# Sums over features as two float32r products, and 64-row products of two heads in turns, in a two-block transformer kernel

## The chip, the cores and the metric

The program runs on one core of a Trainium2 chip. The metric is the device time of one execution in microseconds, the median over runs. A profile of one execution gives the rows below: TensorE is PE (its weight loads PEld), VectorE is DVE, ScalarE is ACT, GpSimd is POOL, and SP issues most of the loads.

## What is computed

Two transformer blocks on 512 tokens of 1024 features, all in float32. Block one is a differential attention with 8 heads, a modulation from a condition vector, and a mixture of 16 experts. Block two is a forgetting attention beside an RWKV-7 recurrence (8 heads of 64), a merge of the two, and a product-key expert layer. What bears on the change:

```python
# block one, per head: rmsnorm over the 128 features of the head
o = rmsnorm(o, subln_g) * (1.0 - lam_init)
# block one: condition rows
mod = cond @ ada_w[i] + ada_b[i]
# block two, recurrence, per head of 64: key norm, bonus, group norm
kk = kk / jnp.maximum(jnp.sqrt(jnp.sum(kk * kk, axis=-1, keepdims=True)), 1e-12)
bonus = jnp.sum(r_h * k_h * r_k.reshape(H, N), axis=-1, keepdims=True) * v_h
mu = jnp.mean(y, axis=-1, keepdims=True)
var = jnp.mean(jnp.square(y - mu), axis=-1, keepdims=True)
```

## The kernel before

Large products are made of three float32r products: each operand is split into a head (`split` L53: an ACT copy that rounds to float32r, L57) and a rest (a DVE subtraction, L58), and `mm3` (L47 to L51) multiplies head by head, rest by head and head by rest. A float32 product is one call, and the trace shows it as two TensorE instructions.

A sum over features is a product with a constant matrix, because features lie on the partitions: `ones` (128 by 128) or `bones` and `bswap` (two blocks of 64 by 64). There are 32 such products of 128 by 512 in float32, each followed by an operation that reads the sum from PSUM:

- `head_norm` (L376): after each of the 8 attention heads, ACT squares the head (L378, tile `sq`), PE sums it (L380), ACT takes logarithm and exponential into `rn` (L382, L383), DVE multiplies (L384) and `rn` is split into `on`, the input of the output projection. The head itself waits in the only PSUM buffer of kind `d` until L384 has read it.
- `ada_end` (L178): 8 sums of half rows of `g1`, `A2`, `B2` and `g2` (L184), read by ACT (L186) or DVE (L188). `g1` is called in the middle of the first half of the output projection (L491), the other three behind it (L499). `A2` and `B2` go through DRAM to the columns that the router uses (L538 to L540, L550).
- `rwkv`, first loop, for each of 4 pairs of heads: the key norm (L1354) and the bonus (L1385).
- `rwkv`, last loop, for each pair: mean (L1562) and variance (L1569) of `y`.

The first loop of `rwkv` (L1346 to L1430) prepares chunks of 32 tokens. Per pair and head, 16 products of 64 by 64 by 64 (L1414, `p` of PSUM kind `a`, which has three buffers) go to DVE masks (L1416, L1417), then to 16 products of 32 rows (L1428). The 16 products read the 64 partitions of their head, and write the lower and the upper 64 partitions of the bank in turns. After the last pair the masked matrices go through DRAM to a triangular recursion on DVE (L1468). Its setting up reuses the loop's memory (L1432 to L1442).

The chain over chunks (L1532) multiplies for both heads in turns (L1537), head 0 from rows 0 to 63 into the lower half and head 1 from rows 64 to 127 into the upper half of one tile. The last loop (L1545) has 15 products of 64 by 64 by 32 for one head and then 15 for the other, into the two halves of one bank (L1553), with one step of the merge's products (`fill(1, fox)`) behind each head; then `y` (L1558, two buffers), the two sums, the scaling (L1570 to L1575) and the split into `yrT`. The loads of `gt` and `bo` for the next pair (L1547, L1548) have one buffer each. Another float32 product with all four quarters of the array in turns is L1522.

No order is written by hand around these places: the tile framework orders the instructions of each engine by program order and by when it reckons them ready, gives tiles of one `tag` the same buffers, and lets a new tile of a tag wait until the one before it is released. PE runs its list in order. `fill` hands it steps of other products between.

Of the kernel before, what the change touches and what calls it, by code (L numbers as in the profile page):

```python
# [27 lines left out]
class Kern:  # L28
# [24 lines left out]
    def split(self, hl, src, scale=None, eng=None):  # L53
# [5 lines left out]
        else:  # L59
            nc.scalar.activation(hl[0], src, AF.Copy, scale=scale)  # L60
            nc.vector.scalar_tensor_tensor(hl[1], src, scale, hl[0].bitcast(F32), OP.mult, OP.subtract)

    def pair(self, pool, shape, tag, bufs=None):
        return [self.t(pool, shape, F32R, tag + s, bufs) for s in ("_hi", "_lo")]
# [45 lines left out]
    def constants(self, cp):  # L110
        nc, I = self.nc, self.I
        self.ident = self.t(cp, [128, 128], F32, "ident")
        nc.vector.memset(self.ident, 0.0)
        nc.gpsimd.affine_select(self.ident, self.ident, pattern=[[-1, 128]], compare_op=OP.not_equal, fill=1.0,
                                base=0, channel_multiplier=1)
        self.ones = self.t(cp, [128, 128], F32, "ones")
        nc.vector.memset(self.ones, 1.0)
        self.cols = self.t(cp, [128, I["cols"].shape[1]], F32, "cols")
        nc.sync.dma_start(self.cols, I["cols"])
        self.acols = self.t(cp, [128, 3 * KC], F32, "acols")  # L120
        nc.sync.dma_start(self.acols, I["acols"])
# [55 lines left out]

    def ada_end(self, dst, gain=None):  # L178

        nc = self.nc  # L180
        for h in range(2):
            s = slice(h * 512, h * 512 + 512)
            p = self.ps(kind="b")
            nc.tensor.matmul(p, self.ones, dst[:, s], start=True, stop=True)  # L184
            if gain is None:
                nc.scalar.activation(dst[:, s], p, AF.Copy)  # L186
            else:
                nc.vector.scalar_tensor_tensor(dst[:, s], p, 1.0, gain[:, s], OP.add, OP.mult)  # L188
# [18 lines left out]
    def mixer1(self):  # L207
        nc, I, tc = self.nc, self.I, self.tc
        with ExitStack() as ph:
# [166 lines left out]
            def head_norm(h, po):  # L376
                sq = self.t(sp, [128, T], F32, "sq", 1)
                nc.scalar.activation(sq, po, AF.Square)  # L378
                pss = self.ps(kind="b")
                nc.tensor.matmul(pss, self.ones, sq, start=True, stop=True)  # L380
                rn = self.t(sp, [128, T], F32, "rn", 1)
                nc.scalar.activation(rn, pss, AF.Ln, bias=epsc, scale=1.0 / 128)  # L382
                nc.scalar.activation(rn, rn, AF.Exp, scale=-0.5)  # L383
                nc.vector.scalar_tensor_tensor(rn, po, gcol, rn, OP.mult, OP.mult)  # L384
                self.split([z[:, h, :] for z in on], rn)
# [94 lines left out]
            nf = nf.rearrange("p a b -> p (a b)")  # L480
            def residual(pool, p, t, h):
                hs = slice(h * 512, (h + 1) * 512)
                y = self.t(pool, [128, 512], F32, "ry", 1)
                nc.vector.tensor_tensor(y, p, self.g1[:, hs], OP.mult)
                nc.vector.tensor_tensor(xr[:, t, hs], xr[:, t, hs], y, OP.add)
# [3 lines left out]
            for kc in range(KC):  # L489
                if kc == 4:  # L490
                    self.ada_end(self.g1)  # L491
                if kc == KC - 1:
                    head_norm(7, po)
                    self.dump("on", on[0].bitcast(F32))
                for t in range(NT):
                    ts = slice(t * 128, (t + 1) * 128)
                    self.mm3(py[t], [z[:, kc, ts] for z in on], [z[:, kc % 2, :] for z in ws[kc // 2]], kc == 0, kc == KC - 1)
            for d, gain in ((self.A2, nf), (self.B2, None), (self.g2, None)):
                self.ada_end(d, gain)  # L499
            for t in range(NT):  # L500
                residual(wo0, py[t], t, 0)
            self.close_right("m1wo")
# [3 lines left out]
            with tc.tile_pool(name="m1wo1", bufs=1) as op:  # L506
                ws = [wout(wp, op, kc, 1, 4) for kc in (0, 2, 4, 6)]
                for t in range(NT):
# [6 lines left out]
                    self.router_half(xr, t, 0)  # L515
                    residual(op, p, t, 1)
                    self.router_half(xr, t, 1)
# [725 lines left out]
    def rwkv(self, xT, yfT, wp):  # L1243
# [11 lines left out]
        with self.rw as ph:  # L1255
# [8 lines left out]
            BA = [self.t(ba, [128, 2, 8, 96], F32, "BA%d" % i) for i in range(4)]  # L1264
            bones, bswap = (self.t(one, [128, 128], F32, "bones%d" % i) for i in range(2))
            for m, i in ((bones, 0), (bswap, 64)):
# [8 lines left out]
            with ExitStack() as sub:  # L1275
# [70 lines left out]
                for hp in range(4):  # L1346
# [6 lines left out]
                    p = self.ps()  # L1353
                    nc.tensor.matmul(p, bones, sq, start=True, stop=True)  # L1354

# [28 lines left out]
                    p = self.ps()  # L1384
                    nc.tensor.matmul(p, bswap, r, start=True, stop=True)  # L1385
                    nc.vector.tensor_tensor(r, p, v, OP.mult)
# [6 lines left out]
                    for n, src in (("bk", bk), ("ar", ar), ("v", v2)):  # L1393
                        for i in range(2):
# [12 lines left out]
                            else:  # L1407
                                nc.vector.tensor_copy(Vr[:, ps_, :], p)
                    for g in range(2):
                        gs, vs = slice(g * 64, (g + 1) * 64), slice(64 - g * 64, 128 - g * 64)  # L1410
                        p = self.ps([128, 8, 2, C])
                        for j in range(16):
                            o = j % 2 * 64
                            nc.tensor.matmul(p[o:o + 64, j // 2], bk[gs, j].rearrange("p i t -> p (i t)"), ar[gs, j].rearrange("p i t -> p (i t)"), start=True, stop=True,  # L1414
                                             tile_position=(g * 64, o))
                        nc.vector.tensor_tensor(AI[g][:, :, 0, :], p[:, :, 0, :], m2[:, 0:1, :].to_broadcast([128, 8, C]), OP.mult)  # L1416
# [34 lines left out]
            def fill(n, steps):  # L1451
                for _ in zip(range(n), steps):
                    pass
# [91 lines left out]
            for hp in range(4):  # L1545
# [3 lines left out]
                p = self.ps([128, 16, C], "c")  # L1549
                for g in range(2):  # L1550
                    gs, vs = slice(g * 64, (g + 1) * 64), slice(64 - g * 64, 128 - g * 64)
                    for j in range(1, 16):
                        nc.tensor.matmul(p[vs, j, :], MW[hp][gs, j - 1, 64:128], rT[gs, hp, j, :], start=True, stop=True,  # L1553
                                         tile_position=(g * 64, 64 - g * 64))
                    fill(1, fox)
                y = self.t(sp, [128, T], F32, "y", 2)
# [481 lines left out]
```

## Time and profile before

| | |
|---|---|
| median of 3 runs | 2536.67 us (2530.67 to 2538.79) |
| the profiled execution | 2533.18 us |
| its span, first to last instruction | 2531.5 us |
| mean granted TensorE clock | 0.982 of full speed |
| PE busy | 2418.7 us, 96% |
| DVE, ACT, POOL busy | 1925.4, 1123.1, 545.8 us |

The last 1271 us are the product-key layer, which the change leaves alone. The places above lie at these times of the span: heads 120 to 286 us, condition rows and output projection 286 to 312, first loop of the recurrence 860 to 978, triangular recursion from 978, chain over chunks 1100 to 1136, last loop 1135 to 1184. A busy PE means that some product is in flight, and the recorded length of a product overlaps the next; what a product costs the queue is the distance of its start to the start of the next.

### The profile page before, as it was taken

How to read it: one execution, taken by the hardware profiler on the slowest of the kernel's cores; microseconds unless marked ns; L12 is line 12 of the kernel's file. 1: busy time of each engine (PE TensorE's matmuls, PEld its weight loads, DVE VectorE, ACT ScalarE, POOL GpSimd, SP SyncE). 2: the span in 40 equal slices, each digit the busy share in tenths (PEclk: the TensorE clock that was granted, in tenths of full speed). 3: DMA queues.
4: the chain of work that ended last, by engine and by line, in shares of the span. 5: the costliest groups of instructions: out<-in, count | busy, mean ns of one | idle time of the engine just before them, and what ended most of it. 6: DMA issues, size and time to landing. Idle time of an engine off the chain costs nothing.

```text
span 2531.5 us, 36170 instructions
## 1 busy us (share of the span) xinstructions
PE 2418.7 (96%) x13502; PEld 1982.1 (78%) x13502; DVE 1925.4 (76%) x3698; ACT 1123.1 (44%) x1651; POOL 545.8 (22%) x456
## 2 busy tenths in 40 slices
PE   8999989999899999999999999989999899999998
PEld 5766766666567687777789989988888789888887
DVE  5577669898866657646689999948787688888886
ACT  3466547777534543223434445533333233333333
POOL 2010112223311100000000000024544434454440
PEclk9999989999999999998999999999999999999999
DMA  7343269999731122213343338799999899999992
GB/s 266 117 172 112 93 223 334 361 369 368 254 104 42 60 77 74 76 55 121 115 140 119 118 103 316 288 385 328 350 347 325 311 332 325 343 333 350 336 330 78
DMA packets 224248, 566.31 MB, mean 224 GB/s; under 512 B 27755, under 2 KB 75924, under 8 KB 223174
## 3 DMA queue, kind: packets, MB, share of 16 engines
q1 hardware_dynamic: 173218, 387.53, 43.5%
q0 software_dynamic: 46048, 166.73, 18.6%
q10 hardware_dynamic: 4804, 9.72, 1.0%
q8 instruction: 107, 1.75, 0.3%
q14 instruction: 71, 0.58, 0.1%
HBM read 511.99 MB, written 51.92 MB: 223 GB/s over the span
## 4 chain that ended last, share of the span: by engine, by line
issue 17%; PE 17%; DVE 10%; POOL 8%; DMA 3%; ACT 0%; POOLq 0%; DVEq 0%; ACTq 0%
POOL row L1765 8%; DMA row<-in_v,ix 2%; PE psu L49 2%; PE psu L51 2%; PE psu L50 2%; PE psx L1750 2%; PE py L50 1%; PE py L51 1%; PE py L49 1%; DVE u_lo L58 1%; PE psb L49 1%; PE psb L51 1%; PE psb L50 1%; DVE eq L1718 1%; DVE ti L1663 1%
## 5 line engine op out<-in xcount | busy, mean ns | idle before, releaser
L49 PE MATMUL psu<-x4T_hi,u_hi 128*128 128x384 f32 x1024 | 346.5, 339 | 5.3 <-ACT act L1815 4.4
L51 PE MATMUL psu<-x4T_hi,u_lo 128*128 128x384 f32 x1024 | 344.4, 337 | 2.3 <-DVE u_lo L58 2.3
L50 PE MATMUL psu<-x4T_lo,u_hi 128*128 128x384 f32 x1024 | 344.1, 336 | 0.0
L50 PE MATMUL py<-v_lo,W_hi 128*128 128x512 f32 x768 | 303.3, 395 | 13.3 <-DVE v_lo L58 13.3
L49 PE MATMUL py<-v_hi,W_hi 128*128 128x512 f32 x768 | 302.1, 393 | 5.8 <-ACT W_hi L57 4.4
L51 PE MATMUL py<-v_hi,W_lo 128*128 128x512 f32 x768 | 302.6, 394 | 4.0 <-DVE W_lo L58 4.0
L57 ACT ACTIVATE W_hi<-act 128x384 fp32r<-128x384 f32 x128 | 66.4, 525 | 395.1 <-DVE act L1899 395.1
L58 DVE TENSOR_TENSOR ew_lo<-ew_raw,ew_hi 128x2048 fp32r<-128x2048 f32 x93 | 216.7, 2331 | 28.4 <-ACT ew_hi L57 28.3
L1765 POOL DMA_INDIRECT row<-in_v,ix x128 | 183.3, 1432 | 220.1 <-DVE x L1781 188.6
L1765 POOL DMA_INDIRECT row<-in_u,ix x128 | 180.7, 1411 | 221.5 <-DVE dots L1772 203.2
L57 ACT ACTIVATE w_hi<-w_raw 128x1024 fp32r<-128x1024 f32 (+1 forms) x103 | 101.9, 992 | 226.3 <-PE psb L50 148.9
L57 ACT ACTIVATE u_hi<-u_raw 128x1024 fp32r<-128x1024 f32 x128 | 135.0, 1057 | 149.3 <-PE psu L50 132.6
L49 PEld LDWEIGHTS psu<-x4T_hi,u_hi 128*128 128x128 f32 x1024 | 193.1, 189 | 9.6 <-ACT act L1815 4.7
L50 PEld LDWEIGHTS psu<-x4T_lo,u_hi 128*128 128x128 f32 x1024 | 193.2, 189 | 3.7
L57 ACT ACTIVATE ew_hi<-ew_raw 128x2048 fp32r<-128x2048 f32 x93 | 178.1, 1916 | 39.2 <-PE psa L51 38.1
L51 PEld LDWEIGHTS psu<-x4T_hi,u_lo 128*128 128x128 f32 x1024 | 192.9, 188 | 2.9 <-DVE u_lo L58 2.8
L1772 DVE CUSTOM_DVE_ANT_0 row<-row,x 128x1024 f32<-128x1024 f32 x128 | 153.2, 1219 | 45.4 <-DMA row<-in_u,ix 45.3
L50 PEld LDWEIGHTS py<-v_lo,W_hi 128*128 128x128 f32 x768 | 145.8, 190 | 46.1 <-DVE v_lo L58 18.6
L58 DVE TENSOR_TENSOR v_lo<-v_raw,v_hi 128x1024 fp32r<-128x1024 f32 x128 | 156.2, 1221 | 33.0 <-ACT v_hi L57 33.0
L1781 DVE SCALAR_TENSOR_TENSOR x<-row,rg,x 128x1024 f32<-128x1024 f32 x128 | 164.0, 1281 | 17.6 <-DMA row<-in_v,ix 15.9
L51 PEld LDWEIGHTS py<-v_hi,W_lo 128*128 128x128 f32 x768 | 146.1, 190 | 35.9 <-DVE W_lo L58 5.6
L49 PEld LDWEIGHTS py<-v_hi,W_hi 128*128 128x128 f32 x768 | 145.7, 190 | 34.7 <-ACT W_hi L57 4.8
(662 smaller groups left out, 5455.0 us busy)
## 6 DMA issues: line engine op xcount, KB each, us to landing
u_raw<-in_uT SPq DMA_DIRECT2D x128, 512.0 KB, 6.1
v_raw<-in_v SPq DMA_DIRECT2D x128, 512.0 KB, 6.5
ew_raw<-in_wgate SPq DMA_DIRECT2D x32, 1024.0 KB, 7.3
ew_raw<-in_wup SPq DMA_DIRECT2D x32, 1024.0 KB, 7.7
ew_raw<-in_wdown SPq DMA_DIRECT2D x32, 1024.0 KB, 9.7
gd<-Gs SPq DMA_DIRECT2D x6, 4096.0 KB, 13.1
G<-gd SPq DMA_DIRECT2D x32, 768.0 KB, 8.8
w_raw<-in_w2b SPq DMA_DIRECT2D x39, 512.0 KB, 3.5
```

The lines of the kernel that those rows point to most:

```text
L49: mm(out, L[0], R[0], start=start, stop=False)
L50: mm(out, L[0], R[1], start=False, stop=False)
L51: mm(out, L[1], R[0], start=False, stop=stop)
L57: nc.scalar.activation(hl[0], src, AF.Copy)
L58: (eng or nc.vector).tensor_tensor(hl[1], src, hl[0].bitcast(F32), OP.subtract)
L1663: nc.vector.max_index(idx[:, 8:16], vals[:, 8:16], rest)
L1718: nc.vector.tensor_tensor(e4, e4, tf[:, s, :, :, None].to_broadcast([128, NT, 16, 16]), OP.mult)
L1750: nc.tensor.matmul(p[:, u, :], A[j], B[i][j], start=i == 0, stop=i == 1)
L1765: keep(nc.gpsimd.indirect_dma_start(r, None, I[name], bass.IndirectOffsetOnAxis(ap=ix[:, h, j:j + 1], axis=0)))
L1772: keep(nc.vector.tensor_tensor_reduce(r, r, x[:, t, :], 1.0, 0.0, OP.mult, OP.add, dots[:, h, j:j + 1]))
L1781: keep(nc.vector.scalar_tensor_tensor(x[:, t, :], r, g[:, h, j:j + 1], x[:, t, :], OP.mult, OP.add))
```

## The change

The sums become two float32r products, of the head and of the rest of the summed operand, with constants held as float32r (`ones_r`, and `bones` and `bswap` themselves). `halves` makes the two parts in buffers of tags that are there already (`rn`, `km`, `r`, `sq`, `kk`) or new (`sql`, `yh`, `yl`), one buffer each. To make room for `sql`, the scratch of the first four `residual` calls moves from the pool of the weights to tag `a`. The products L1414 and L1553 of the two heads of a pair are issued in turns; for L1414 the upper and lower output halves of head 1 are swapped in order, so that neighbours share neither rows nor columns, and both heads' PSUM tiles are open at once. The two steps of `fill` in the last loop come behind both heads.

```diff
+    def halves(self, pool, x, tags):
+        hl = [self.t(pool, [128, T], F32R, tag, 1) for tag in tags]
+        self.split(hl, x)
+        return hl
+    def sums(self, out, m, hl):
+        self.nc.tensor.matmul(out, m, hl[0], start=True, stop=False)
+        self.nc.tensor.matmul(out, m, hl[1], start=False, stop=True)
...
+        self.ones_r = self.t(cp, [128, 128], F32R, "ones_r")
+        nc.vector.tensor_copy(self.ones_r, self.ones)
...
-            nc.tensor.matmul(p, self.ones, dst[:, s], start=True, stop=True)
+            self.sums(p, self.ones_r, self.halves(pool, dst[:, s], ("rn", "sql")))
...
-                nc.tensor.matmul(pss, self.ones, sq, start=True, stop=True)
+                self.sums(pss, self.ones_r, self.halves(sp, sq, ("rn", "sql")))
...
-                residual(wo0, py[t], t, 0)
+                residual(sp, ("a", 2), py[t], t, 0)
...
-                    nc.tensor.matmul(p, bones, sq, start=True, stop=True)
+                    self.sums(p, bones, self.halves(sp, sq, ("km", "r")))
...
-                    nc.tensor.matmul(p, bswap, r, start=True, stop=True)
+                    self.sums(p, bswap, self.halves(sp, r, ("sq", "kk")))
...
+                    pg = [self.ps([128, 8, 2, C]) for _ in range(2)]
+                    for j in range(16):
+                        for g in range(2):
+                            gs, i = slice(g * 64, (g + 1) * 64), j ^ g
+                            o = i % 2 * 64
+                            nc.tensor.matmul(pg[g][o:o + 64, i // 2], bk[gs, i].rearrange("p i t -> p (i t)"), ar[gs, i].rearrange("p i t -> p (i t)"), start=True, stop=True,
+                                             tile_position=(g * 64, o))
                     for g in range(2):
...
-                        p = self.ps([128, 8, 2, C])
-                        for j in range(16):
-                            o = j % 2 * 64
-                            nc.tensor.matmul(p[o:o + 64, j // 2], bk[gs, j].rearrange("p i t -> p (i t)"), ar[gs, j].rearrange("p i t -> p (i t)"), start=True, stop=True,
-                                             tile_position=(g * 64, o))
...
-                for g in range(2):
-                    gs, vs = slice(g * 64, (g + 1) * 64), slice(64 - g * 64, 128 - g * 64)
-                    for j in range(1, 16):
+                for j in range(1, 16):
+                    for g in range(2):
+                        gs, vs = slice(g * 64, (g + 1) * 64), slice(64 - g * 64, 128 - g * 64)
                         nc.tensor.matmul(p[vs, j, :], MW[hp][gs, j - 1, 64:128], rT[gs, hp, j, :], start=True, stop=True,
                                          tile_position=(g * 64, 64 - g * 64))
-                    fill(1, fox)
+                fill(2, fox)
...
-                nc.tensor.matmul(p, bones, y, start=True, stop=True)
+                self.sums(p, bones, self.halves(sp, y, ("yh", "yl")))
...
-                nc.tensor.matmul(p, bones, sq, start=True, stop=True)
+                self.sums(p, bones, self.halves(sp, sq, ("yh", "yl")))
```

## Rows read from the trace of the kernel before

**Rows 1.** The page's first part: busy time and share of each engine.
```profile
PE 2418.7 (96%) x13502; PEld 1982.1 (78%) x13502; DVE 1925.4 (76%) x3698; ACT 1123.1 (44%) x1651; POOL 545.8 (22%) x456
```

**Rows 2.** Busy time by stretch: length, each engine, granted clock, DMA share, GB/s.
```profile
120.00:286.00 166.00, 162.39 (x876) 113.17 (x875) 121.86 (x293) 108.61 (x219) 12.83 (x19) 0.98 0.39 137
286.00:312.00 26.00, 26.00 (x97) 17.90 (x97) 12.81 (x18) 9.94 (x15) 6.16 (x21) 1.00 0.15 25
860.00:978.00 118.00, 118.00 (x988) 92.09 (x987) 65.61 (x103) 55.55 (x92) 4.04 (x12) 1.00 0.24 77
978.00:1030.00 52.00, 45.21 (x196) 36.09 (x194) 47.67 (x71) 13.95 (x18) 4.85 (x6) 0.99 0.21 71
1135.00:1180.00 45.00, 45.00 (x340) 33.54 (x337) 22.75 (x44) 13.14 (x21) 3.24 (x6) 0.85 0.23 65
```

**Rows 3.** Timeline of PE in the last loop: start, length, line, shapes, count.
```profile
1161.24 0.39 PE L51 MATMUL psb<-yfT_hi,w_lo 128*128 128x512 f32 x1
1161.47 1.02 PE L1562 MATMUL psa<-y,bones 128*128 128x512 f32 x2
1162.42 1.93 PE L1553 MATMUL psc<-rT,X 64*64 64x32 f32 x30
1164.29 0.50 PE L49 MATMUL psb<-yfT_hi,w_hi 128*128 128x512 f32 x1
```

**Rows 4.** Groups by line, 1135 to 1184: busy, mean ns, idle before.
```profile
L1553 PE MATMUL psc<-rT,X 64*64 64x32 f32 x240 | 17.2, 231 | 0.0
...
L58 DVE TENSOR_TENSOR yrT_lo<-y,yrT_hi 128x512 fp32r<-128x512 f32 x4 | 2.8, 692 | 3.6 <-ACT yrT_hi L57 3.4
...
L57 ACT ACTIVATE yrT_hi<-y 128x512 fp32r<-128x512 f32 x4 | 2.5, 628 | 1.2 <-DVE y L1575 1.2
```

**Rows 5.** Timeline of PE: float32 products of 64 rows in three places.
```profile
889.56 1.15 PE L1414 MATMUL psa<-ar,bk 64*64 64x64 f32 x32
...
1055.34 1.14 PE L1522 MATMUL psc<-X,BA 64*64 64x64 f32 x58
...
1131.45 0.28 PE L1537 MATMUL psc<-X 64*64 64x64 f32 x4
1131.57 0.28 PE L1537 MATMUL psa<-X 64*64 64x64 f32 x4
```

**Rows 6.** Timeline of PE: the last products of the recurrence's first loop.
```profile
975.78 1.15 PE L1428 MATMUL psa<-Vr,AI 32*64 32x64 f32 x32
```

**Rows 7.** Busy time by short stretches of the last loop, columns as in rows 2.
```profile
1137.00:1139.00 2.00, 2.00 (x37) 2.00 (x35) 0.00 (x0) 0.00 (x0) 0.00 (x0) 0.84 0.49 126
...
1143.00:1145.00 2.00, 2.00 (x8) 1.05 (x6) 0.96 (x2) 0.70 (x2) 0.00 (x0) 0.50 0.00 0
...
1165.00:1167.00 2.00, 2.00 (x23) 1.82 (x21) 0.73 (x2) 0.00 (x0) 0.00 (x0) 0.66 0.76 183
...
1171.00:1173.00 2.00, 2.00 (x7) 1.41 (x6) 1.24 (x2) 0.61 (x1) 0.00 (x0) 0.63 0.00 0
```

**Rows 8.** Timeline of DVE, last pair of heads: first and last step of its chain.
```profile
1168.26 0.66 DVE L1558 TENSOR_TENSOR y<-psc,yi 128x480 f32<-128x480 f32 x1 [2.49 <-PE psc L1553]
...
1183.13 0.69 DVE L58 TENSOR_TENSOR yrT_lo<-y,yrT_hi 128x512 fp32r<-128x512 f32 x1
```

**Rows 9.** Waits, 120 to 286: total us, times, longest.
```profile
PEld psb L380 <- ACT sq L378: 4.6, 7, 1.1
```

**Rows 10.** Timeline of PE around the condition rows.
```profile
295.37 2.07 PE L184 MATMUL psb<-A,ones 128*128 128x512 f32 x4
297.28 1.03 PE L184 MATMUL psb<-B,ones 128*128 128x512 f32 x2
297.93 0.61 PE L49 MATMUL psd<-w_hi,on_hi 128*128 128x512 f32 x1
```

**Rows 11.** Timeline of DVE in the same place.
```profile
297.04 0.74 DVE L384 SCALAR_TENSOR_TENSOR rn<-psd,gcol,rn 128x512 f32<-128x512 f32 x1
...
298.48 0.69 DVE L58 TENSOR_TENSOR on_lo<-rn,on_hi 128x512 fp32r<-128x512 f32 x1
```

More of the change, by code (lines that the diff above doesn't have):

```diff
@@ L176, in ada_rows, with ada_end @@
         yield
-    def ada_end(self, dst, gain=None):
+    def ada_end(self, pool, dst, gain=None):
         nc = self.nc
@@ L480, in mixer1, with residual @@
             nf = nf.rearrange("p a b -> p (a b)")
-            def residual(pool, p, t, h):
+            def residual(pool, scratch, p, t, h):
                 hs = slice(h * 512, (h + 1) * 512)
-                y = self.t(pool, [128, 512], F32, "ry", 1)
+                y = self.t(pool, [128, 512], F32, *scratch)
                 nc.vector.tensor_tensor(y, p, self.g1[:, hs], OP.mult)
@@ L490, in mixer1 @@
                 if kc == 4:
-                    self.ada_end(self.g1)
+                    self.ada_end(sp, self.g1)
                 if kc == KC - 1:
@@ L498, in mixer1 @@
             for d, gain in ((self.A2, nf), (self.B2, None), (self.g2, None)):
-                self.ada_end(d, gain)
+                self.ada_end(sp, d, gain)
             for t in range(NT):
-                residual(wo0, py[t], t, 0)
+                residual(sp, ("a", 2), py[t], t, 0)
             self.close_right("m1wo")
@@ L515, in mixer1 @@
                     self.router_half(xr, t, 0)
-                    residual(op, p, t, 1)
+                    residual(op, ("ry", 1), p, t, 1)
                     self.router_half(xr, t, 1)
@@ L1264, in rwkv @@
             BA = [self.t(ba, [128, 2, 8, 96], F32, "BA%d" % i) for i in range(4)]
-            bones, bswap = (self.t(one, [128, 128], F32, "bones%d" % i) for i in range(2))
-            for m, i in ((bones, 0), (bswap, 64)):
+            bones, bswap = (self.t(one, [128, 128], F32R, "bones%d" % i) for i in range(2))
+            for m, i in ((bones.bitcast(F32), 0), (bswap.bitcast(F32), 64)):
                 nc.gpsimd.memset(m, 0.0)
@@ L1408, in rwkv @@
                                 nc.vector.tensor_copy(Vr[:, ps_, :], p)
-                    for g in range(2):
-                        gs, vs = slice(g * 64, (g + 1) * 64), slice(64 - g * 64, 128 - g * 64)
-                        p = self.ps([128, 8, 2, C])
-                        for j in range(16):
-                            o = j % 2 * 64
-                            nc.tensor.matmul(p[o:o + 64, j // 2], bk[gs, j].rearrange("p i t -> p (i t)"), ar[gs, j].rearrange("p i t -> p (i t)"), start=True, stop=True,
-                                             tile_position=(g * 64, o))
+                    pg = [self.ps([128, 8, 2, C]) for _ in range(2)]
[5 more added lines that the diff above has]
+                                             tile_position=(g * 64, o))
+                    for g in range(2):
+                        gs, vs, p = slice(g * 64, (g + 1) * 64), slice(64 - g * 64, 128 - g * 64), pg[g]
                         nc.vector.tensor_tensor(AI[g][:, :, 0, :], p[:, :, 0, :], m2[:, 0:1, :].to_broadcast([128, 8, C]), OP.mult)
@@ L1549, in rwkv @@
                 p = self.ps([128, 16, C], "c")
-                for g in range(2):
-                    gs, vs = slice(g * 64, (g + 1) * 64), slice(64 - g * 64, 128 - g * 64)
-                    for j in range(1, 16):
+                for j in range(1, 16):
+                    for g in range(2):
+                        gs, vs = slice(g * 64, (g + 1) * 64), slice(64 - g * 64, 128 - g * 64)
                         nc.tensor.matmul(p[vs, j, :], MW[hp][gs, j - 1, 64:128], rT[gs, hp, j, :], start=True, stop=True,
                                          tile_position=(g * 64, 64 - g * 64))
-                    fill(1, fox)
+                fill(2, fox)
                 y = self.t(sp, [128, T], F32, "y", 2)
```

## The prediction

> **What bounds the kernel now.** I read the page's first part, the busy time by stage, the timelines of PE, DVE and ACT in the stages that the change touches, and the waits there. PE is busy for 96% of the span [rows 1], and in four of the five stretches concerned for 98 to 100% of the stretch, with DVE and ACT at 30 to 75% [rows 2]: there PE's queue sets the pace, and time taken from it counts if nothing else comes late. The exception is the recursion from 978, where DVE has 47.7 of 52 us and PE gaps [rows 2]; for that stage only its start counts. The fifth stretch, 1135 to 1180, has a granted clock of 0.85 [rows 2], and this is two dips: the clock falls to 0.50, the lower level of 1.2 GHz, within 1137 to 1139 and within 1165 to 1167 and comes back at 1145 and within 1171 to 1173 [rows 7]; each time PE has just worked through 56 to 60 instructions of L1553 with hardly another product between.
>
> **What one sum costs.** A product of 128 by 512 in float32r takes PE's queue 0.23 us (1161.24 to 1161.47), and the float32 sum behind it 0.95 us (1161.47 to 1162.42) [rows 3]. Two float32r products should take 0.46. That leaves up to 0.49 per sum; some of the 0.95 is the change to the next kind of product, so I take 0.43, and for 32 sums 13.8 us of PE. What is added is an ACT copy (0.63) and a DVE subtraction (0.69) [rows 4], 1.3 us plus a handoff ahead of each sum, say 1.4. In busy time that is 20 us on ACT and 22 on DVE, which have room [rows 2]. In a chain that somebody waits for it is 1.4 - 0.43, about 1 us to the bad.
>
> **What the turns save.** L1414, which changes columns but not rows, takes 1.15/32 = 36 ns an instruction; L1522, of the same size but with all four quarters of the array in turns, 1.14/58 = 20 ns; L1537, two opposite quarters, four in 0.12 us = 30 ns; L1553, always the same quarter, 1.87/30 = 62 ns (1162.42 to 1164.29) [rows 3, 5]. The new order of L1414 visits four quarters, that of L1553 two opposite ones. So L1414: 256 instructions x 16 ns = 4.1 us; L1553: 240 x 32 ns = 7.7 us. The least is nothing (no overlap at all).
>
> The Trainium skill speaks against L1553: "TensorEngine Tiling (Array Packing)", section "Gotcha 1: PSUM Pressure", says that different row tiles cannot use one PSUM bank at once, and here both heads write one bank. By it L1553 would stay at 62 ns. The trace disagrees for L1537, whose two row groups also fill two halves of one tile, at 30 ns [rows 5]; I go by that row and keep the rule as a rival.
>
> **Stage by stage, against the profiled 2533.2 us.**
> Heads: 7 sums x 0.43 = 3.0 us of PE. But PE waits already for `sq` before each of them, 4.6 us in 7 waits on the weight load [rows 9], and the halves come in there; the framework will put the sum later in the list, behind other projections, but its reckoning is not exact. From +3 to -7 us (7 x 1); I take 1.5 saved, since PE has the projections of coming heads to fill with, and since nobody needs `on` before the output projection. The PSUM buffer of the head is released up to 1.4 us later; the next head writes it one tile (166/32 = 5.2 us) or more later, which covers this.
> Condition rows: today three of the sums (295.37 to 297.93) fill the time in which PE waits for L384 to free the buffer `d` [rows 10, 11]. With halves they cannot: `rn` is occupied by the last head until `on` is split at 299.2 [rows 11]. So PE stands idle there for 2.5 us, as good as free today, and the six sums of `A2`, `B2` and `g2` come behind, one after the other because `rn` and `sql` have one buffer, some 2.1 us each (0.63 + 0.69 + 0.46 + handoffs), to about 312. PE pays six times 0.46, as much as the three at 0.95 that it pays behind 297.93 now; the two of `g1` and the last head's save 1.3. `B2` reaches the router some 1 us later, while PE has three tiles of output projection left. Between +4 and -6; I take +1. The moved scratch has two buffers for one and costs nothing.
> First loop of the recurrence: 8 x 0.43 + 4.1 = 7.5 us of PE. Each sum needs an operand that ACT or DVE has just made, but the next projections (24 products x 0.23 = 5.5 us each) may be pulled ahead of it, two at a time. At the end both heads' masks can follow at once, so the last L1428 [rows 6] ends some 2 us earlier, of which 1 is new; the set-up of the recursion waits for that memory. 8.5 at best, -3 if each sum waits fully for its halves; I take 7. Having two tiles of L1414 open takes two of three buffers of kind `a`, and L1428 the third; the next user is the next pair's sum, at least one projection later.
> Last loop: PE loses 7.7 for the turns and 8 x 0.43 = 3.4 for the sums. At the lower clock, where products take twice as long, it spends 0.32 x 2 x 2 us before 1139, 6 to 1145, and 1.4, 4 and 1.5 us from 1165 to 1173 (shares by the clock of [rows 7]), 14 us in all, so 7 us are lost to it, L1553's own included (17.2 us against 240 x 62 ns = 14.9 [rows 4]). With half the time in such products, and neighbours in other quarters, I expect no dip. PE alone could thus give 18 us. But then the chain of `y` is next: the last pair's goes from 1168.3 to 1183.8, 15.5 us [rows 8], gets 2.7 longer by two splits and 2 shorter without the dip. If L1553 of that pair ends 14 us earlier (what PE saves before it), the chain ends 13 earlier; one buffer for `yh`, `yl` and `ysq` and the loads of `bo` make pairs queue, so I take 11. From 3 (sums alone) to 18. `fill` moved behind both heads issues the same two steps: nothing.
> One copy into `ones_r` at the start lies beside the first loads: nothing.
>
> Sum: 1.5 + 1 + 7 + 11 = 20.5 us, 2533.2 - 20.5 = 2512.7. The profiled execution was 3.5 us under the median of 2536.67, so the forecast is 2516. A difference under 0.3%, 7.6 us, can't be told from none.
>
> **The rivals.**
> *The turns of L1553 don't overlap*, since both heads write one bank. Then its 62 ns stay and so do the dips; the last loop gives 3. 12.5 us saved, 2524. Against it: L1537 at 30 ns [rows 5]; for it: L1553's products are half as wide as L1537's, so a fixed cost per product could weigh more. 0.12. (For it speaks also the Trainium skill, "TensorEngine Tiling (Array Packing)", in the section named above.)
> *The chain of `y` takes over early*: pairs queue at the single buffers, PE runs dry and its clock may fall while it waits. For it: today chain and PE end within a microsecond of each other [rows 8]. The last loop then gives 5, in all 14.5, 2522. 0.18.
> *The sums wait for their halves* (slower). PE's list keeps every sum where it is, directly behind its operand, and PE stands for the 1.4 us of copy and subtraction, 32 times: 32 x (1.4 - 0.43) = 31 us lost, against 15 that the turns give (4 + 11): 2552. It decides from a mean wait of 0.43 + 15/32 = 0.9 us a sum. For it: the 0.7 us waits of today at `sq` [rows 9]; against it: PE has no such wait worth naming elsewhere, since the framework orders by readiness. 0.08.
> *The change doesn't reach PE's list*: products are again bunched by head because the framework orders them so, and the sums' gain is eaten by small waits. 2534. 0.07.
>
> **How the numbers follow.** The forecast holds 0.55, with 2507 to 2525 for its own bounds (last loop 18 for 11 and the heads' 3 for 1.5 on one side; on the other 9 less). The range has to take in the two rivals at 2522 and 2524 with their own spread and half of the unchanged case: 2505 to 2533. Faster by over 0.3% (below 2529) needs the forecast or the first two rivals, 0.85, less what their lower ends spill: 0.80. Slower: the waiting sums, less their milder outcomes: 0.06. The rest, 0.14, is within.
>
> **What would show it.** Right: the sums as two products 0.23 us apart; L1414 near 20 ns and L1553 near 30 ns an instruction, 1.9 us per pair; a granted clock of 1.0 all through the last loop; PE gaps of some 2.5 us before 298; the last loop 9 to 13 us shorter, the first one 6 to 8, the heads 0 to 3. Wrong: waits of PE's weight load for rests (L58) ahead of the sums that add up to over 10 us; L1553 still at 62 ns; a late `yrT_lo` with PE idle before it at a low clock; or a later first product of the expert layer because the rows `B2` came late.

## Result, and the profile after

The changed kernel takes 2551.52 us (median of five runs) where the kernel before takes 2534.97 on the same chip: a ratio of 1.0076, 95% interval 1.0061 to 1.0092. The medians differ by 16.5 us, which alone is a ratio of 1.0065; the interval holds both figures. The forecast was some 20 us faster, with a range that ends at 2533.

The first part of the page, after [rows 1]:

```profile
PE 2406.4 (94%) x13502; PEld 1973.5 (77%) x13502; DVE 1946.6 (76%) x3731; ACT 1141.1 (45%) x1683; POOL 549.7 (22%) x456
```

PE is busy for 12.3 us less, as the change wants, while the span has grown by 17.8 (2531.5 to 2549.3). So about 30 us of new idle time came in. The busy time by stretch, columns as in [rows 2], shows where:

```profile
286.00:312.00 26.00, 21.08 (x74) 14.67 (x72) 11.79 (x19) 7.31 (x12) 2.42 (x11) 0.86 0.00 0
312.00:330.00 18.00, 8.64 (x23) 5.42 (x23) 4.37 (x4) 6.81 (x10) 4.97 (x10) 0.69 0.81 225
330.00:374.00 44.00, 33.08 (x175) 27.51 (x175) 23.47 (x72) 15.04 (x33) 7.12 (x3) 0.81 0.27 97
...
1157.00:1180.00 23.00, 23.00 (x305) 18.10 (x304) 15.90 (x28) 11.17 (x17) 1.09 (x2) 1.00 0.24 70
1180.00:1198.00 18.00, 13.25 (x48) 9.16 (x47) 15.14 (x26) 8.71 (x14) 2.15 (x4) 0.91 0.62 219
```

From 286 to 330 PE works 29.7 of 44 us, at a granted clock that falls to 0.69; before, it worked 26 of the first 26 at 1.00. The last loop shows no dip any more (1.00, where the 45 us of [rows 2] have 0.85), but behind 1180 PE runs out of work.

Landmarks of every run that follows, read from the start times in its trace (us): the router's mask product, the first L1414, the first L1553, the last `yrT_lo`, the last product that reads it, and the span. Lines are those of the kernel before. The last column is the ratio of times to the kernel before, measured beside each run, with its interval.

```
run                          mask  L1414   L1553  yrT_lo  product   span   ratio
before                      348.1  884.1  1135.7  1183.1  1202.6  2531.5
after                       373.3  909.9  1157.0  1197.5  1219.4  2549.3  1.0076 [1.0061, 1.0092]
e1_rows_one_product         361.4  898.3  1148.1  1188.7  1211.2  2541.6  1.0051 [1.0034, 1.0068]
e2_rows_only                375.1  911.6  1162.3  1205.2  1224.7  2556.2  1.0117 [1.0097, 1.0136]
e3_recurrence_only          347.7  884.3  1131.4  1172.0  1192.6  2518.8  0.9993 [0.9980, 1.0007]
e4_rows_other_pool          367.4  904.1  1151.2  1191.7  1212.3  2538.5  1.0069 [1.0050, 1.0088]
e5_scratch_only             366.2  901.5  1152.2  1195.1  1214.5  2545.6  1.0060 [1.0039, 1.0081]
e6_held_loads               362.6  900.5  1147.2  1187.7  1208.7  2538.4  1.0052 [1.0035, 1.0069]
e7_turns_only               347.6  883.1  1132.1  1165.8  1186.9  2518.3  0.9959 [0.9944, 0.9974]
e8_sums_only                347.6  885.6  1139.6  1187.1  1207.7  2542.6  1.0052 [1.0033, 1.0071]
e9_rows_scratch_back        372.8  909.4  1158.9  1199.4  1222.1  2553.6  1.0078 [1.0056, 1.0099]
e10_heads_and_recurrence    343.5  881.2  1128.4  1169.0  1189.7  2521.6  0.9983 [0.9969, 0.9997]
e11_rows_own_memory         361.0  897.7  1144.8  1185.2  1207.1  2533.5  1.0026 [1.0013, 1.0038]
e12_heads_and_turns         346.2  883.0  1132.1  1165.7  1186.8  2518.0  0.9955 [0.9939, 0.9971]
```

Between before and after the mask product moves by +25.2 us, the first L1414 by +25.8, the first L1553 by +21.3 (the first loop and the recursion gain 4.5), the last `yrT_lo` by +14.4 (the last loop gains 6.9), the product behind it by +16.8. The loss lies ahead of the mask product, in the stage of the condition rows. The part of the span behind the last product differs by up to 8.7 us among these executions (1326.2 to 1334.9), and a profiled execution need not be a typical one: those of e3 and e4 are the fastest of their runs, 6.4 and 6.6 us under the medians, and that of the kernel before stands 2 to 4 us above the medians beside e1 to e12. So gains and losses in time are read from the ratios, and the landmarks for the place and length of single stages.

What stood at that place before, from its timelines, and from its view of transfers (the last number is microseconds from issue to landing):

```profile
299.31 1.06 ACT L57 ACTIVATE w_hi<-w_raw 128x1024 fp32r<-128x1024 f32 x1 [0.37 <-DVE on_lo L58]
299.65 0.40 ACTq L540 DMA_DIRECT2D abcols<-abd  x1
300.19 0.94 POOL L531 DMA_DIRECT2D wr<-in_rgw  x1
309.08 0.38 ACTq L540 DMA_DIRECT2D abcols<-abd  x1
311.89 0.92 SPq L740 DMA_DIRECT2D ew_raw<-in_wgate  x2
```

```profile
abcols<-abd ACTq DMA_DIRECT2D x2, 4.0 KB, 2.2
```

The same events after:

```profile
294.35 0.79 PE L49 MATMUL psd<-w_hi,on_hi 128*128 128x512 f32 x1 [2.22 <-DVE rn L397]
303.68 0.39 PE L71 MATMUL psb<-rn,ones_r 128*128 128x512 f32 x1
309.27 0.80 PE L71 MATMUL psb<-rn,ones_r 128*128 128x512 f32 x1 [1.21 <-ACT rn L57]
314.46 0.80 PE L72 MATMUL psb<-sql,ones_r 128*128 128x512 f32 x1
317.90 1.65 PE L49 MATMUL psa<-w_hi,on_hi 128*128 128x512 f32 x3 [2.64 <-ACT w_hi L57]
334.70 0.61 PE L567 MATMUL psb<-bw,ones 128*128 128x20 f32 x2 [10.22 <-DVE bw L565]
...
316.79 2.95 ACT L57 ACTIVATE w_hi<-w_raw 128x1024 fp32r<-128x1024 f32 x3 [0.90 <-issue]
315.66 1.08 ACTq L553 DMA_DIRECT2D abcols<-abd  x2
315.56 0.94 POOL L544 DMA_DIRECT2D wr<-in_rgw  x1 [18.77 <-PE psb L72]
315.29 0.92 SPq L753 DMA_DIRECT2D ew_raw<-in_wgate  x2
333.85 0.44 DVE L563 TENSOR_TENSOR x1T<-wr,abcols 128x160 f32<-128x160 f32 x1 [12.29 <-DMA abcols<-abd]
```

Two things went wrong one behind the other. Everything that takes over the attention pool's memory (the second half of the output weights, the router's small tiles) started at 299.3 to 300.2 before, right behind the last head's `on_lo`; now it starts at 315.6 to 316.8, behind the last sum of a row (314.46). The column transfer of `B2` also waits for its row, whose write to DRAM goes out at 311.55 for 307.77 before. And the 4 KB transfers of the columns of `A2` and `B2` (L553), which used to go out before any expert load (299.65 and 309.08 against 311.89), are now issued in the same microsecond as the 1 MB expert weights: DVE can use them at 333.85, some 17 us after their issue, where they landed after 2.2 us before, and PE stands 10.22 us for it.

### The profile page after: what moved, and what is told of

It is laid out like the page before. It is cut to its first block, busy times and chain, and to the rows that moved or that the text cites. A ratio compares the mean times of both kernels' runs of the same rounds, so it can differ in the third digit from the quotient of the medians.

```text
span 2549.3 us, 36258 instructions
## 1 busy us (share of the span) xinstructions
PE 2406.4 (94%) x13502; PEld 1973.5 (77%) x13502; DVE 1946.6 (76%) x3731; ACT 1141.1 (45%) x1683; POOL 549.7 (22%) x456
## 4 chain that ended last, share of the span: by engine, by line
PE 27%; issue 19%; DVE 13%; POOL 8%; DMA 5%; ACT 1%; POOLq 0%; DVEq 0%; SPq 0%; ACTq 0%
POOL row L1781 8%; PE psb L49 3%; PE psb L51 2%; PE psb L50 2%; DMA row<-in_v,ix 2%; PE psu L49 2%; PE psu L51 2%; PE psu L50 2%; PE psx L1766 2%; PE py L50 1%; PE py L51 1%; DVE u_lo L58 1%; PE py L49 1%; DVE w_lo L58 1%; PE psa L49 1%
```

## The experiments

### The condition rows

**e1**, the rows' sums as one product again, everything else of the change kept:

```diff
-            self.sums(p, self.ones_r, self.halves(pool, dst[:, s], ("rn", "sql")))
+            nc.tensor.matmul(p, self.ones, dst[:, s], start=True, stop=True)
```

> The kernel after, with the eight sums of the condition rows (ada_end) back to one float32 product each; everything else of the change stays. Theory A (the rows' halves hold the attention pool's memory about 16 us longer, so the second half of the output weights starts late and the small transfer of the columns of A and B falls among the expert weights: about 25 us lost before 374 us): the first second-half product starts near 307 us again, the router's mask product (373.3 us in the kernel after, 348.1 before) near 348 to 353, and the time is 2525 to 2533 us, below the kernel before. Rival B (every one of the 32 sums waits about 1 us for its halves, all over the kernel): the six or eight us of these sums alone go, 2543 to 2546. Rival C (the moved scratch of the first-half residual alone holds that memory): no change from the kernel after, 2548 to 2553.

**e4**, the rows' halves in a pool that outlives the attention:

```diff
-            self.sums(p, self.ones_r, self.halves(pool, dst[:, s], ("rn", "sql")))
+            hl = self.t(pool, [128, 2, 512], F32R, "w_raw", 3)
+            hl = [hl[:, 0], hl[:, 1]]
+            self.split(hl, dst[:, s])
+            self.sums(p, self.ones_r, hl)
...
-                self.ada_end(sp, d, gain)
+                self.ada_end(wp, d, gain)
```

> The kernel after, with the rows' halves in the pool of the weights (one tile of 128x2x512, three buffers) that outlives the attention, instead of in two single buffers of the attention's pool. The arithmetic is that of the kernel after. Theory A: the attention's memory is freed as in the kernel before, the second half starts near 307 to 309 us, the transfer of the columns is issued before the expert weights, the mask product stands near 350 us, time 2524 to 2532. Rival B: no change, 2548 to 2553. Between the two, near 2540: the memory counts, but so does the chain of splits and sums by itself.

Theory A's numbers were missed by both: e1 took 2541.96 and e4 2546.79 against 2529.5 for the kernel before, and the ratio of e4 can't be told from that of the kernel after. Both kept the moved scratch. In e1 the second half starts in time (307.3), so the halves did hold that memory back; but DVE still waits 11.1 us for the columns and the mask product stands at 361.4. Something besides the halves makes the columns late.

**e2**, the opposite: the kernel before with `ada_end` on halves and the moved scratch, nothing else.

> The kernel before with the rows' halves and the moved scratch alone (heads and recurrence untouched). Theory A: the whole loss is here, the router's mask product near 373 us, time 2555 to 2562 (2535 plus 25, less what later idle stretches give back). Rival B: eight sums of about 1 us each, 2540 to 2545. If only the transfer's collision were made by the shift of this run's timing: somewhere between, with the transfer of the columns landing within 4 us of its issue.

2558.57, 29 us above before, mask product at 375.1: the whole loss is made by these edits. **e5** does the scratch alone:

```diff
-                residual(wo0, py[t], t, 0)
+                residual(sp, ("a", 2), py[t], t, 0)
```

> The kernel before with one edit: the first-half residual's scratch moves from the output weights' pool to the attention's pool (tag a, two buffers). No sum is touched. Theory S (formed from the run with the rows as one product, which kept this move and lost 12.5 us): the weights' pool, whose memory the first expert weights take over, is now free before the residuals end, and the attention's pool, whose memory the router's small tiles take over, only after them; the small transfer of the columns of A and B is issued together with the 1 MB loads and lands 10 us or more after its issue, the router's mask product stands near 360 us instead of 348, time 10 to 15 us above the kernel before of the same chip (near 2540 to 2545). Rival: the scratch is one buffer among many and what delayed the columns in the other runs was the change's shift in time; then within 0.2 per cent of before, columns landing 2 us after their issue.

2545.75 against 2531.21, 14.5 us above, and no sum was touched. Its timeline (SP's queue, ACT's, DVE, PE):

```profile
309.88 0.92 SPq L740 DMA_DIRECT2D ew_raw<-in_wgate  x2
309.92 0.44 ACTq L540 DMA_DIRECT2D abcols<-abd  x1
327.14 0.44 DVE L550 TENSOR_TENSOR x1T<-wr,abcols 128x160 f32<-128x160 f32 x1 [11.97 <-DMA abcols<-abd]
327.99 0.62 PE L554 MATMUL psb<-bw,ones 128*128 128x20 f32 x2 [10.85 <-DVE bw L552]
```

Before, the scratch sat in the output weights' pool and so kept the expert loads, which take over that memory, back until the last residual (311.89), while the columns could go from 299.65. With the scratch in the attention's pool both wait for the same release and leave 0.04 us apart. Here the expectation held: 10 to 15 us were expected of the scratch alone.

**e9** keeps the rows' halves and puts the scratch back (for room, the second half takes tag `a` instead of the new `sql`):

```diff
-                residual(sp, ("a", 2), py[t], t, 0)
+                residual(wo0, py[t], t, 0)
```

> The kernel after with the scratch of the first-half residual back in the output weights' pool; the rows' halves stay in the attention's pool (for room the second half, in heads and rows, takes the existing tag a instead of a new tile). Theory S plus halves: the expert weights wait again for the last residual, so the columns land within 4 us of their issue; the halves still free the attention's memory late, so the second half of the output weights starts near 317 us as in the kernel after. The loss before the mask product is then 8 to 12 us instead of 25, and the time 0 to 5 us above the kernel before of the same chip. If the columns' delay came from the late halves alone: no change from the kernel after, 15 to 20 us above before.

A miss: 2550.39, 19.2 us above, mask product at 372.8, columns and first expert loads 0.4 us apart. Timelines of SP, ACT and POOL:

```profile
314.96 0.92 SPq L753 DMA_DIRECT2D ew_raw<-in_wgate  x2
315.34 1.08 ACTq L553 DMA_DIRECT2D abcols<-abd  x2
315.23 0.94 POOL L544 DMA_DIRECT2D wr<-in_rgw  x1 [19.00 <-PE psb L72]
```

I had taken it that the loads would still wait for the residuals. They do, but those end at 309.3, and SP's queue then waits, like the router's load in the last line, for PE's last half sum (L72): the loads' memory also overlaps the attention's, which the halves hold until 315. So either edit alone brings the two transfers together. With both, the mask product comes little later than with the halves alone (373.3 in the kernel after against 372.8), and 8.9 us later than with the scratch alone (375.1 in e2 against 366.2).

**e6** tells the collision from the late release. The kernel after, but the first four expert loads wait for the columns:

```diff
+                if early is not None or (e, which) == (0, 1):
+                    for i in range(2):
+                        nc.gpsimd.tensor_copy(raw[:, 0, i:i + 1], self.abcols[:, i, 0:1])
                 nc.sync.dma_start(raw, src)
```

> The kernel after, but the first four expert loads (1 MB each) wait until the columns of A and B have landed (two one-column copies by GpSimd from the columns into each load's buffer ahead of it, overwritten by the load). Theory S: the columns land within 4 us of their issue instead of 18, DVE's wait for them (12.3 us) and TensorE's 10.2 us wait behind it go, the mask product moves from 373 to 361 to 365 us, and the time is 6 to 11 us below the kernel after, so 6 to 11 us above before. Rival (the columns are slow for another reason, such as their own many small packets or the other small transfers of the router issued in the same microsecond): the columns still take over 10 us and the time stays or grows.

2542.25, 11.0 us above before where the kernel after was 16.5 above; the mask product at 362.6. Its transfers, then its timeline:

```profile
abcols<-abd ACTq DMA_DIRECT2D x2, 4.0 KB, 3.9
```

```profile
316.35 1.03 ACTq L553 DMA_DIRECT2D abcols<-abd  x2
322.12 0.44 DVE L563 TENSOR_TENSOR x1T<-wr,abcols 128x160 f32<-128x160 f32 x1
322.85 0.37 SPq L756 DMA_DIRECT2D ew_raw<-in_wgate  x1
```

With no expert load beside them the columns land in 3.9 us, and DVE does not wait for them. The collision thus cost 10.7 us at the mask product. Against e10, which has the same heads without the rows' edits, the kernel after is 29.8 us late there (373.3 against 343.5); the other 19.1 stand beside the late release and the later loads, and no run takes these two apart. The trace after shows what the columns are made of: between 300 and 345 us ACT's queue moved 2084 packets for 0.02 MB, so each of the two transfers is about a thousand packets of a few bytes. The Trainium skill, "DMA: Bandwidth & Descriptors", section "Queues, rings and completion order", says that a DMA engine takes turns between its queues a whole packet at a time; by that each small packet stands behind a large one. The runs agree with it: DVE gets the same bytes 16 us after their issue in e5 (of the two transfers the trace dates one landing there, after 11.3 us), and they land after 3.9 in e6.

**e11** tries all sums of the change with neither hold: e4's shared tile, the scratch back, `a` for the heads' second half.

> All of the change's sums, with neither hold on the attention's memory: the rows' halves in one tile of the weights' pool (three buffers), the residual's scratch back in the output weights' pool, the heads' second half in the existing tag a. Theory (what counts is that the attention's pool ends with the last head, ahead of the expert loads): the columns land within 4 us of their issue, no wait of DVE for them, the mask product stands between 343 and 353 us, time 6 below to 2 above the kernel before of the same chip. Rival (the serial splits of the rows cost by themselves, memory or not): 3 to 8 us above before, with TensorE waiting for the halves. If it were the number of buffers of the shared tile: the weights' load waits on it, and the second half of the output starts late though the columns come early.

2535.83 against 2528.91, 6.9 above, and 12.8 worse than the same without the rows' halves (e10, 5.9 below). The columns' wait is down to 5.2 us, but the weights' loads now queue for the shared tile. Timeline of ACT:

```profile
309.17 1.06 ACT L57 ACTIVATE w_hi<-w_raw 128x1024 fp32r<-128x1024 f32 x1 [2.08 <-DMA w_raw<-in_wout]
```

The first of these stood at 299.31 before. The late weights are the third case of its expectation, but the columns don't come early: the first go at 298.50, the second, of `B2`, at 309.23, behind an expert load of 308.52, and DVE has them at 319.36. The time, 6.9, also lies in the range of its rival (3 to 8, the splits cost by themselves), but PE doesn't wait for halves there: it waits 3.6 us for the late weights and 3.0 for the columns. What the rows' halves would cost in memory of their own stays open; it was not tried.

### The recurrence

**e10**: the change without its edits of the rows' stage (heads and recurrence alone).

> The kernel after without its two edits of the condition rows' stage: rows as one product each, scratch back in the weights' pool. What stays are the heads' sums (second half in tag a) and the recurrence. Theory: nothing is lost before 374 us, the heads gain 1 to 3 us, the first loop 2 to 4, the last loop up to 8 less what the merge gives back: 4 to 12 us below the kernel before of the same chip, 2518 to 2526. Rival (sums cost their halves): at or above the kernel before.

2525.31, 5.9 below before, within the expectation: the only ratio so far whose interval lies below 1. **e3** has the recurrence alone:

> The kernel before with the recurrence's part of the change alone: its sums as two products, and the 64-row products of both loops in turns. Theory A: all that the change gains except the heads, 2535 less about 3.4 (first loop) less 7.8 (last loop) plus up to 3.4 given back in the merge: 2523 to 2530. Rival B: 24 sums of about 1 us each cost more than the turns gain, 2537 or more. In the trace of this run the condition rows look as in the kernel before.

2526.96, 2.5 below, and the interval holds 1. So a gain in time is not shown for it, and 18 us can be excluded. **e7** and **e8** take e3 apart: the turns with float32 sums, and the sums as halves with the products in their old order.

> The kernel before with the turns of the 64-row products in both loops of the recurrence alone; all sums one float32 product. Theory T (the turns carry the recurrence's gain, the sums' halves give back in the chain of y what they take off TensorE): 3 to 9 us below before of the same chip, and in the last loop the last half of y is ready no later than in the run of the recurrence alone. Rival (the sums carry it): within 2 us of before. In the last loop TensorE should lose the 60 ns per product: 30 products of the last pair in about 0.95 us instead of 1.87.

> The kernel before with the recurrence's sums as two products alone, the 64-row products as before. Theory T: 2 us below to 3 us above before of the same chip: TensorE is spared about 0.4 us on each of 16 sums at most, and the chains of the two loops grow by a split (1.4 us) per sum. Rival (the prediction's price, 0.43 to 0.5 us of TensorE saved per sum and all of it on the path): 6 to 8 us below before.

e7: 2519.47, 9.4 below, just past its range. e8: 2543.88, 15.0 *above*, worse than either case of its expectation. The turns carry the gain, and the sums cost. By stages: from the first to the last L1414 the kernel before takes 90.6 us, e7 87.7, e8 93.9 and e3 85.9 (85.8 to 85.9 in all eight executions that have this loop). From the first L1414 to the first L1553 they take 251.6, 249.0, 254.0 and 247.1, which says less, since the eight range from 246.7 to 249.8. From there to the last `yrT_lo` they take 47.4, 33.7, 47.5 and 40.6.

The 47.4 are more than the loop needs. In e2 and e5, whose recurrence is that of the kernel before, the same way takes 42.9 us, at a mean granted clock of 0.96 over its first 45 us, where the kernel before has 0.85. Busy time by stretch in e5, columns as in [rows 2]:

```profile
1152.20:1176.20 24.00, 24.00 (x236) 18.31 (x235) 11.96 (x22) 7.25 (x11) 1.09 (x2) 1.00 0.21 56
1180.20:1184.20 4.00, 4.00 (x14) 2.55 (x13) 1.07 (x2) 1.32 (x2) 0.00 (x0) 0.57 0.25 97
```

So of the 13.7 us between the kernel before and e7, 4.5 are a dip of the clock that e5 lost without an edit of this loop, and the turns give 9.2, what is left of the dip in e5 included. The sums alone cost 4.6 (e8 against e5; in e8 the clock is 1.00 through all of L1553), and beside the turns 6.9 (e3 against e7).

Why, in the last loop: the last pair's chain in e7 and in e3, DVE and PE.

```profile
1153.59 0.65 DVE L1561 TENSOR_TENSOR y<-psc,yi 128x480 f32<-128x480 f32 x1
1155.19 1.02 PE L1565 MATMUL psa<-y,bones 128*128 128x512 f32 x2
1158.16 1.12 PE L1572 MATMUL psa<-ysq,bones 128*128 128x512 f32 x2
1165.75 0.69 DVE L58 TENSOR_TENSOR yrT_lo<-y,yrT_hi 128x512 fp32r<-128x512 f32 x1
```

```profile
1158.37 0.66 DVE L1574 TENSOR_TENSOR y<-psc,yi 128x480 f32<-128x480 f32 x1
1160.86 0.50 PE L71 MATMUL psa<-yh,bones 128*128 128x512 f32 x1 [0.31 <-ACT yh L57]
1165.03 0.51 PE L71 MATMUL psa<-yh,bones 128*128 128x512 f32 x1 [1.11 <-ACT yh L57]
1171.98 0.69 DVE L58 TENSOR_TENSOR yrT_lo<-y,yrT_hi 128x512 fp32r<-128x512 f32 x1 [0.70 <-ACT yrT_hi L57]
1172.01 0.73 PE L49 MATMUL psb<-yrT_hi,w_hi 128*128 128x512 f32 x2 [2.57 <-ACT yrT_hi L57]
```

In e3 the last L1553 ends earlier (1150.2 against 1152.2), yet its `y` is added up 4.8 us later. In both runs this follows closely on the `yrT_lo` of the second pair, which frees one of the two buffers of `y` (it starts at 1157.09 in e3 and at 1152.78 in e7): the pairs ahead are slower. That the one buffer each of `yh`, `yl` and `ysq` makes them so is argued, not tested. And from there to `yrT_lo` it takes 13.6 us against 12.2. At the end PE is out of work and waits 2.57. The kernel after shows the same rows:

```profile
1190.58 0.51 PE L71 MATMUL psa<-yh,bones 128*128 128x512 f32 x1 [1.09 <-ACT yh L57]
1197.50 0.72 PE L49 MATMUL psb<-yrT_hi,w_hi 128*128 128x512 f32 x2 [2.73 <-ACT yrT_hi L57]
```

In the first loop PE is never idle before or in e8, so there the sums cost PE time itself. The groups by line of that loop, before and in e8 (one float32 sum counts as two instructions):

```profile
L1414 PE MATMUL psa<-ar,bk 64*64 64x64 f32 x254 | 10.4, 223 | 0.0
L1354 PE MATMUL psa<-sq,bones 128*128 128x512 f32 x6 | 3.4, 644 | 0.0
```

```profile
L1427 PE MATMUL psa<-ar,bk 64*64 64x64 f32 x256 | 13.9, 227 | 0.0
L72 PE MATMUL psa<-kk,bones 128*128 128x512 f32 x4 | 2.0, 502 | 0.0
L71 PE MATMUL psa<-sq,bones 128*128 128x512 f32 x4 | 2.0, 501 | 0.0
```

A sum is 3.4/3 = 1.13 us before and 0.50 + 0.50 in halves; but the 64-row products, the same in number and order, are now busy for 3.5 us longer. The timeline says why: counted over the loop, L1414 runs in 12 pieces before and in 24 in e8, with half sums, transposes (L1411) and the products of 32 rows between. The timeline of PE after:

```profile
909.48 0.49 PE L71 MATMUL psa<-sq,bones 128*128 128x512 f32 x1
909.90 0.34 PE L1428 MATMUL psa<-ar,bk 64*64 64x64 f32 x8
910.18 1.09 PE L1411 MATMUL psc<-ident,ar 128*128 128x128 f32 x8
911.20 0.33 PE L1428 MATMUL psa<-ar,bk 64*64 64x64 f32 x4
911.47 0.50 PE L72 MATMUL psa<-kk,bones 128*128 128x512 f32 x1
911.90 0.45 PE L1428 MATMUL psa<-ar,bk 64*64 64x64 f32 x14
```

Pieces of 4 to 14 products stand between products of 128 rows, and a half takes 0.42 us from its start to the next start here (909.48 to 909.90), not 0.23. Four products take 0.27 us that way (911.20 to 911.47), 68 ns each. The Trainium skill, "TensorEngine Tiling (Array Packing)", section "Key Properties", says that a change of tiling mode drains TensorE; the rows agree that each change costs.

Against the profile of the kernel before, e8's shows 5.1 us up to the last product of the recurrence, with the dip of 4.5 us hidden in that difference, and 6.0 behind it, where nothing was edited; that part is not explained.

**e12** is the version that drops what cost: the heads' sums and the turns, everything else as before.

> The candidate for a version that beats both kernels: the heads' sums as two products (second half in tag a) and the turns of both loops; rows, scratch and the recurrence's sums as in the kernel before. Theory T: 5 to 12 us below before of the same chip, at or below the run with heads and the whole recurrence (5.9 below). Rival (sums of the recurrence gain on TensorE): 1 to 4 us above that run, 2 to 5 below before.

2518.72 against 2528.91, ratio 0.9955 [0.9939, 0.9971]: 10.2 us faster than the kernel before, and so faster than both kernels. As a version it keeps the heads' sums, but against e7 they add nothing that the runs can tell; their mask product is 1.4 us earlier (346.2 against 347.6).

## Why the prediction was wrong

**Condition rows, "I take +1", from -6 to +4: this term failed.** The runs show 25.2 us lost at the mask product, the heads' gain already taken off, and e2, which has the edits of this stage alone, takes 29.1 us more than the kernel before. The mechanics were read rightly up to a point: PE's gap before 294.35 is 2.22 us for the forecast 2.5, and the sums came one after another, to 314.5 for "about 312". The row of `B2` goes out 3.8 us later (311.55 against 307.77). The failing step is the one that priced only PE: "PE pays six times 0.46" and "`B2` reaches the router some 1 us later". The halves' buffers are the last users of the attention's memory, and I did not ask what takes that memory over. The second half of the output weights does (first product 317.90), and the router's tiles.

**"The moved scratch has two buffers for one and costs nothing": failed.** It costs 14.5 us alone (e5). I counted buffers and not what the old place held back: by keeping the output weights' pool it had kept the expert loads behind the columns' transfers.

**Turns of L1553, 62 to about 30 ns: right; no dip: right, but not shown to come from the turns.** One run of 52 in the kernel after, on PE's timeline:

```profile
1157.25 1.68 PE L1569 MATMUL psc<-rT,X 64*64 64x32 f32 x52
```

That is (1.68 - 0.22)/51 = 29 ns, with 0.22 the length of one, both heads writing one bank. The rule that I kept as a rival, of the Trainium skill, "TensorEngine Tiling (Array Packing)", section "Gotcha 1: PSUM Pressure", does not show here: by it these products would have stayed at 62 ns. The granted clock is 1.00 through these products. It is also 1.00 through all of L1553 in e8, in the old order, and in e5 through the run of 56 that starts at 1152.47, the same run within which the clock fell in the kernel before. So such a run alone does not bring the dip, and 4.5 of the 7 us reckoned for the dips were missing in e5 without an edit of the loop. (In the sum for them 0.32 x 2 x 2 has a 2 too many; with 0.64 the total is 13.5 us for 14, which changes little.)

**Last loop, 11 saved, from 3 to 18: 6.9 at `yrT_lo`, 4.5 at the product behind it.** Of the 6.9, 4.5 are the dip that e5 lost too; against e5's 42.9 us the loop saves 2.4. The chain of `y` did take over, as the second rival said. The mis-sized term is what two splits a pair and single buffers add to it: 2.7 us were reckoned for the last pair's splits and 2 for the queueing (13 to 11), 6.9 were measured over the loop (e3 against e7).

**First loop, 7 saved: 4.7 from the first to the last L1414.** The turns give 2.9 (e7) for the 4.1 reckoned: L1414 stands in 16 pieces where I had one run at 20 ns, and is busy for 7.7 us, 30 ns an instruction (in the kernel after 20 pieces and 8.7 us, 34 ns). The sums' 3.4 became -3.3 alone (e8) and +1.8 beside the turns (e3 against e7).

**Heads, 1.5 saved:** 1.4 at the mask product by e12 against e7, 4.2 by e10 against e3; right within what single executions tell.

The rival in which each sum waits for its halves gave 2552, and 2551.52 came. Its number fits and its mechanism does not: PE's waits at the sums come to 2.7 us in the heads (1.8 before, at `sq`), 3.7 in the rows and 2.0 at the tail, not 1 us at each of 32. That the two agree is chance. I had asked of each edit what it does to PE's queue, and of none whose memory it keeps.

## What to carry to other kernels

When a tile moves to another pool, or a new one is put into a pool that is about to end, list what takes over that memory and which transfers stand behind it: here one scratch tile set the order of two transfers, worth 14.5 us. Splitting operands for a faster product paid little here even where PE is the bound: beside the turns it gave 1.8 us in the first loop and cost 6.9 in the last, where a chain waits for the halves, and alone it cost 3.3 and 4.6. The same 64-row products in turns, which cost no other engine anything, gave 9.4 us by themselves. A change of several edits is best timed edit by edit: a gain of 10 us was in it. And before a dip of the clock is priced, look whether another execution of the same code has it.

## What was not expected of the hardware

A 4 KB transfer of about a thousand packets landed after 2.2 to 3.9 us with no expert load beside it; issued together with 1 MB loads it reached DVE after 16 to 17 us. A half sum of 128 by 512 takes 0.23 us among its like and 0.42 next to 64-row products. PE's clock was low in the kernel after where it had stood idle most: 0.69 over 312 to 330 us, with PE busy for 8.64 of 18. But in the last loop the same run of 56 small products was followed by a clock of 0.50 in the kernel before and of 1.00 in e5, with PE busy throughout in both.
